# Placing a table of eight constants and padding small tables, so that every large tile of a decoder trunk starts at a multiple of 128 bytes in SBUF

## The chip, the cores and the metric

The kernel runs on one core of a Trainium2 chip. The metric is the device time of one execution in microseconds (us); the time of a kernel is the median of its runs. Five engines work side by side: TensorE (PE, whose weight loads the profile lists as PEld), VectorE (DVE), ScalarE (ACT), GpSimd (POOL) and SyncE (SP), which here only issues DMAs. SBUF is the on-chip memory; a tile takes the same byte range in each of its partitions, and all offsets below are byte offsets within a partition.

## The reference

A trunk of two layers on x of 512 tokens by 1024 features, in float32. Each layer has three post-norm steps: a SwiGLU feed-forward net (FFN), a mixer, and a second FFN.

```python
def swiglu_ffn(x, w_gu, w_down):
    a, u = jnp.split(x @ w_gu, 2, axis=-1)
    return (jax.nn.silu(a) * u) @ w_down
...
def hybrid_mixer(x, w_in, w_out, sinks, rope_cos, rope_sin, ret_cos, ret_sin):
    h = x @ w_in
    ...
    y_attn = sliding_window_sink_attention(qa, ka, va, sinks)
    ...
    y_ret = multiscale_retention(qr, kr, vr.reshape(B, S, RET_HEADS, HEAD_DIM), gr)
    return jnp.concatenate([y_attn, y_ret], axis=-1) @ w_out
...
    for l in range(DEPTH):
        x = layer_norm(DEEPNORM_ALPHA * x + 0.5 * swiglu_ffn(x, ffn1_w_gu[l], ffn1_w_down[l]),
                       ln1_g[l], ln1_b[l])
        x = layer_norm(DEEPNORM_ALPHA * x + hybrid_mixer(x, w_in[l], w_out[l], attn_sinks[l],
                                                         rope_cos, rope_sin, ret_cos, ret_sin),
                       ln2_g[l], ln2_b[l])
        x = layer_norm(DEEPNORM_ALPHA * x + 0.5 * swiglu_ffn(x, ffn2_w_gu[l], ffn2_w_down[l]),
                       ln3_g[l], ln3_b[l])
```

The hidden width of the FFN is 2816. The mixer has 8 attention heads with a window of 128 tokens and 8 retention heads, all of width 64.

## The kernel before

**Split products.** A float32 operand is split into a high part of type float32r and a low part, the rest (`split`, lines 167 to 172: ACT copies, DVE subtracts). `mm3` (lines 180 to 185) multiplies two split operands with three matmuls: high by high (L183), low by high (L184), high by low (L185), all added in one PSUM bank. In the profile's names of a matmul, `ps<-xh,uh`, the tile named first moves through the array and the second is stationary; each matmul loads its own weights.

**Tiles.** x lies transposed in `xh` and `xl` (16 KB a partition each). Weights come by DMA into two raw buffers of 8 KB and are split into units `uh` and `ul` of 4 KB, six buffers of each. `Weights` hands them out in a fixed order and loads ahead: up to six units are made before the one that PE takes. `small` holds the statistics of the norms and of attention, a few numbers a partition each.

**FFN.** For most of the 11 column blocks `glu7` forms the gate and up projections with seven products of half size instead of eight. Its moving tiles have 256 columns: slices of xh and xl in six of its 14 products, and `Th`, `Tl`, sums of slices of x, in the other eight; the units are stationary. Other blocks use `glu`, where xh moves with 256 or 512 columns. The down projection also uses seven products, in five groups of 12 matmuls each (`seventh`); there the units move with 512 columns and the hidden activations, split into xh and xl as scratch, are stationary. Between products a DMA issued on POOL (L389) adds further weights onto the tile R. A tail (`down`) takes the last two rows of blocks, with tiles `hr`, then follows `norm`.

**Mixer.** Projections as above (`proj`, `proj_tok`), then attention and retention in generators that are stepped between the matmuls of the projections, then the output projection (`half`), whose moving tiles are `b` for the first half. Transposes (L476) multiply by `ident`, which moves; so do the first matmuls of the kernel (L468, `warm`).

**Order and waits.** The order of the instructions on an engine is the program's; splits and matmuls of `mm3` are held to it. Waits between engines follow from the tiles' reads and writes. A tile of a pool waits for the last user of the buffer it takes.

**Where the tiles lie.** Pools lie one behind the other in the order in which they are opened, and each tile is rounded up to 32 bytes. `base` comes first: `ident` (512 bytes), `mhalf` (32), xh, xl, Y (16 KB each). Behind it lie the raw buffers (2 of 8 KB), the units (12 of 4 KB) and `small` (nine kinds of tile, three buffers each: 64 bytes for `st`, 32 for each other, 960 in all). Behind `small` come the pools of the stage: those of an FFN (hT, S, Th, Tl, Q, later R, hr and the tail's units), or those of the mixer, which begin with the tables: cos and sin of 2048 bytes, band 1024, causal and diag 512 each, rsc 128, `sk` and `nsk` 32 each. All other tiles have sizes that are multiples of 128 bytes.

`mhalf` holds the exponent -0.5 eight times. It is written once (L119) and read by POOL for the inverse square roots of the norms (L508) and of retention (L1086). `sk` holds the eight sinks of a layer, `nsk` their negatives; attention reads them in L989 and L991.

Of the kernel before, what the change touches and what calls it, by code (L numbers as in the profile page):

```python
# [7 lines left out]
F32 = mybir.dt.float32  # L8
# [10 lines left out]
P = 128  # L19
# [27 lines left out]
class Weights:  # L47


    def __init__(self, T, items):  # L50
        self.T, self.items = T, items
        self.emitted = self.taken = self.out = 0
        self.ready = []
        self.raws = {}
        self.last = {raw: i for i, (raw, _, _, _) in enumerate(items)}
# [44 lines left out]
class Trunk:  # L100
    def __init__(self, tc, ctx):
        self.tc, self.nc = tc, tc.nc
        self.n = 0
        self.now = 0
        self.pin = True
        self.tasks = []
        self.later = []
        self.pace = None
        self.halves = 2
        nc = self.nc  # L110
        self.base = ctx.enter_context(tc.tile_pool(name="base", bufs=1))
        self.rawp = ctx.enter_context(tc.tile_pool(name="rawp", bufs=2))
        self.unit = ctx.enter_context(tc.tile_pool(name="unit", bufs=UBUFS))
        self.small = ctx.enter_context(tc.tile_pool(name="small", bufs=3))
        self.psum = ctx.enter_context(tc.tile_pool(name="psum", bufs=8, space=PSUM))
        self.ident = self.base.tile([P, P], F32, name="ident")
        make_identity(nc, self.ident)
        self.mhalf = self.base.tile([P, 8], F32, name="mhalf")
        nc.vector.memset(self.mhalf, -0.5)  # L119
        self.xh = self.base.tile([P, KC, SEQ], F32R, name="xh")  # L120
        self.xl = self.base.tile([P, KC, SEQ], F32R, name="xl")
        self.Y = self.base.tile([P, NT, D], F32, name="Y")
# [688 lines left out]
    def mixer(self, sinks, cst, g, b):  # L811
        nc, tc, W = self.nc, self.tc, self.W
        with ExitStack() as ctx:
            cp = self.cpool = ctx.enter_context(tc.tile_pool(name=self.nm("mixc"), bufs=1))
            pool = self.mpool = ctx.enter_context(tc.tile_pool(name=self.nm("mix"), bufs=1))
            self.c = {}
            c = self.c

            def const(name, tag=None):
                ap = cst[name]  # L820
                c[name] = cp.tile(list(ap.shape), F32, tag=tag or name, name=self.nm(name))
                nc.sync.dma_start(c[name], ap)
# [2 lines left out]
            const("ropeS", "sin")  # L825
            for name in ("band", "causal", "diag", "rsc"):
                const(name)
            sk = c["sk"] = cp.tile([P, 8], F32, name=self.nm("sk"))
            nc.sync.dma_start(sk, sinks.partition_broadcast(P))
            c["nsk"] = cp.tile([P, 8], F32, name=self.nm("nsk"))  # L830
            nc.vector.tensor_scalar_mul(c["nsk"], sk, -1.0)

            self.kT = [self.tmp("qk", 6, F32R) for _ in range(2)]
# [354 lines left out]
```

## Time and profile before

| what | value |
|---|---|
| median of 3 runs | 1766.99 us |
| lowest, highest run | 1766.74, 1767.35 us |
| profiled execution, span from first to last instruction | 1765.1 us |
| mean granted TensorE clock in the span | 0.998 |
| instructions in the span | 29166 |
| HBM read, written | 212.38 MB, 2.10 MB |

The time of the profiled execution that the profile gives is its span; the runs' times also hold what lies around it. The page gives the busy time of each engine, groups of instructions by line with count, busy time and mean duration of one, and the chain of work that ended last. Durations of successive matmuls overlap on PE, so the mean duration of one is not the time that each adds. A view of all engines by stretches shows the course of the work: gate and up projections until about 220 us, down projection until about 340, mixer until about 560, then the second FFN, and the same again for the second layer.

### The profile page before, as it was taken

How to read it: one execution, taken by the hardware profiler on the slowest of the kernel's cores; microseconds unless marked ns; L12 is line 12 of the kernel's file. 1: busy time of each engine (PE TensorE's matmuls, PEld its weight loads, DVE VectorE, ACT ScalarE, POOL GpSimd, SP SyncE). 2: the span in 40 equal slices, each digit the busy share in tenths (PEclk: the TensorE clock that was granted, in tenths of full speed). 3: DMA queues.
4: the chain of work that ended last, by engine and by line, in shares of the span. 5: the costliest groups of instructions: out<-in, count | busy, mean ns of one | idle time of the engine just before them, and what ended most of it. 6: DMA issues, size and time to landing. Idle time of an engine off the chain costs nothing.

```text
span 1765.1 us, 29166 instructions
## 1 busy us (share of the span) xinstructions
PE 1752.7 (99%) x11930; PEld 1600.5 (91%) x11930; DVE 1414.9 (80%) x1975; ACT 928.1 (53%) x1456; POOL 182.9 (10%) x152
## 2 busy tenths in 40 slices
PE   9999999999999999999999999999999999999998
PEld 9999988887789999998899999889877899999886
DVE  7888888856767888878888888888567587888887
ACT  5455556378712455555535555554795234555561
POOL 0000022111111000014000000311011110000131
PEclk9999999999999999999999999999999999999999
DMA  6234389422222243369423334982233122334891
GB/s 191 97 96 133 131 202 199 131 85 88 73 79 72 74 137 102 97 208 214 140 68 99 121 96 147 211 203 91 85 95 96 48 95 97 97 96 132 211 218 48
DMA packets 163765, 216.34 MB, mean 123 GB/s; under 512 B 5168, under 2 KB 116528, under 8 KB 163632
## 3 DMA queue, kind: packets, MB, share of 16 engines
q1 hardware_dynamic: 141872, 172.55, 30.5%
q0 software_dynamic: 21760, 41.95, 13.1%
q8 instruction: 93, 1.52, 0.3%
q14 instruction: 40, 0.33, 0.1%
HBM read 212.38 MB, written 2.10 MB: 122 GB/s over the span
## 4 chain that ended last, share of the span: by engine, by line
PE 90%; issue 6%; DMA 1%; DVE 1%; POOL 1%; ACT 0%; SPq 0%; POOLq 0%; DVEq 0%
PE ps L183 29%; PE ps L185 29%; PE ps L184 29%; PE ps L476 1%; DMA raw<-in_ffn_w_gu_dram 1%; POOL sw L959 1%; PE ps L1067 1%; PE ps L1015 0%; PE ps L1029 0%; PE ps L1063 0%; PE ps L1050 0%; DMA retS<-c_retS_dram 0%; ACT sw L957 0%; DVE ul L169 0%; PE ps L1007 0%
## 5 line engine op out<-in xcount | busy, mean ns | idle before, releaser
L183 PE MATMUL ps<-xh,uh 128*128 128x256 f32 (+1 forms) x1616 | 482.2, 298 | 0.0
L185 PE MATMUL ps<-xh,ul 128*128 128x256 f32 (+1 forms) x1616 | 479.3, 297 | 1.0 <-DVE ul L169 0.9
L184 PE MATMUL ps<-xl,uh 128*128 128x256 f32 (+1 forms) x1616 | 478.5, 296 | 0.3 <-DVE xl L169 0.3
L168 ACT CAST uh<-raw 128x1024 fp32r<-128x1024 f32 (+1 forms) x274 | 237.1, 886 | 245.6 <-PE ps L184 140.1
L169 DVE TENSOR_TENSOR ul<-raw,uh 128x1024 fp32r<-128x1024 f32 (+1 forms) x274 | 273.3, 1013 | 62.2 <-ACT uh L168 61.6
L183 PE MATMUL ps<-Th,uh 128*128 128x256 f32 x1152 | 319.1, 277 | 0.0
L184 PE MATMUL ps<-Tl,uh 128*128 128x256 f32 x1152 | 318.7, 277 | 0.0
L185 PE MATMUL ps<-Th,ul 128*128 128x256 f32 x1152 | 318.3, 276 | 0.0
L185 PEld LDWEIGHTS ps<-xh,ul 128*128 128x128 f32 x1616 | 307.9, 191 | 10.1 <-DVE ul L169 1.6
L183 PEld LDWEIGHTS ps<-xh,uh 128*128 128x128 f32 x1616 | 307.9, 191 | 9.7 <-issue 1.6
L184 PEld LDWEIGHTS ps<-xl,uh 128*128 128x128 f32 x1616 | 308.0, 191 | 7.9 <-DVE xl L169 0.5
L183 PE MATMUL ps<-uh,xh 128*128 128x512 f32 x720 | 283.4, 394 | 0.5 <-ACT xh L168 0.5
L185 PE MATMUL ps<-uh,xl 128*128 128x512 f32 x720 | 280.8, 390 | 0.0
L184 PE MATMUL ps<-ul,xh 128*128 128x512 f32 x720 | 280.3, 389 | 0.0
L168 ACT CAST uh<-S 128x1024 fp32r<-128x1024 f32 x144 | 151.1, 1049 | 149.0 <-PE ps L184 145.2
L169 DVE TENSOR_TENSOR ul<-S,uh 128x1024 fp32r<-128x1024 f32 x144 | 175.9, 1222 | 60.1 <-ACT uh L168 59.5
L184 PEld LDWEIGHTS ps<-Tl,uh 128*128 128x128 f32 x1152 | 216.7, 188 | 0.0
L183 PEld LDWEIGHTS ps<-Th,uh 128*128 128x128 f32 x1152 | 216.6, 188 | 0.0
L185 PEld LDWEIGHTS ps<-Th,ul 128*128 128x128 f32 x1152 | 216.4, 188 | 0.0
L389 POOL DMA_DIRECT2D R<-in_ffn_w_down_dram x80 | 97.1, 1217 | 1020.7 <-DVE ul L169 930.0
L169 DVE TENSOR_TENSOR ul<-R,uh 128x1024 fp32r<-128x1024 f32 x120 | 145.1, 1221 | 25.8 <-ACT uh L168 25.7
L183 PEld LDWEIGHTS ps<-uh,xh 128*128 128x128 f32 x720 | 135.2, 188 | 30.1 <-issue 1.6
(143 smaller groups left out, 2362.4 us busy)
## 6 DMA issues: line engine op xcount, KB each, us to landing
raw<-in_ffn_w_gu_dram SPq DMA_DIRECT2D x86, 1024.0 KB, 5.5
R<-in_ffn_w_down_dram POOLq DMA_DIRECT2D x80, 512.0 KB, 7.6
raw<-in_w_in_dram SPq DMA_DIRECT2D x18, 1024.0 KB, 5.2
R<-in_ffn_w_down_dram SPq DMA_DIRECT2D x16, 1024.0 KB, 6.3
raw<-in_ffn_w_down_dram SPq DMA_DIRECT2D x12, 1024.0 KB, 7.2
R<-in_ffn_w_down_dram SPq DMA_DIRECT2D x8, 512.0 KB, 4.3
raw<-in_w_in_dram SPq DMA_DIRECT2D x8, 512.0 KB, 6.1
raw<-in_w_out_dram SPq DMA_DIRECT2D x8, 512.0 KB, 6.4
```

The source lines that it names most:

```text
L168: a = self.nc.scalar.copy(hi, src)
L169: b = self.low = self.nc.vector.tensor_sub(lo, src, hi.bitcast(F32))
L183: keep(mm(out, ah, bh, start=start, stop=False, **kw))
L184: keep(mm(out, ah, bl, start=False, stop=False, **kw))
L185: keep(mm(out, al, bh, start=False, stop=stop, **kw))
L389: self.nc.gpsimd.dma_start(src, rows(i, j, g * 2, 2), accum_op=ALU.add))
L476: nc.tensor.transpose(b[:, c * P : (c + 1) * P], src[:, c * P : (c + 1) * P], self.ident)
L959: nc.gpsimd.tensor_mul(sw[:, :n], sw[:, :n], S)
L1067: ins = nc.tensor.matmul(ob[:, o0 : o0 + HD], ST[h][:, n, :], vr[:, n, p * P + h * HD : p * P + (h + 1) * HD], start=n == 0, stop=n == 0 o ...
```

## The change

`mhalf` leaves the pool `base` for the pool `small`, with one buffer of its own and 16 floats (64 bytes) instead of 8. `sk` and `nsk` are taken 16 floats wide, of which the first 8 are used. Counted from the start of `ident`, xh then lies at 512 bytes instead of 544; `small` has 1024 bytes instead of 960; the mixer's tables from rsc on take 256 bytes instead of 192. Everything else is the same text.

```diff
@@ -115,7 +115,7 @@
         self.ident = self.base.tile([P, P], F32, name="ident")
         make_identity(nc, self.ident)
-        self.mhalf = self.base.tile([P, 8], F32, name="mhalf")
+        self.mhalf = self.small.tile([P, 16], F32, tag="mhalf", name="mhalf", bufs=1)
         nc.vector.memset(self.mhalf, -0.5)
         self.xh = self.base.tile([P, KC, SEQ], F32R, name="xh")
...
@@ -825,9 +825,9 @@
             for name in ("band", "causal", "diag", "rsc"):
                 const(name)
-            sk = c["sk"] = cp.tile([P, 8], F32, name=self.nm("sk"))
+            sk = c["sk"] = cp.tile([P, 16], F32, name=self.nm("sk"))[:, :8]
             nc.sync.dma_start(sk, sinks.partition_broadcast(P))
-            c["nsk"] = cp.tile([P, 8], F32, name=self.nm("nsk"))
+            c["nsk"] = cp.tile([P, 16], F32, name=self.nm("nsk"))[:, :8]
             nc.vector.tensor_scalar_mul(c["nsk"], sk, -1.0)
```

## The prediction

> **What bounds the kernel now.** I read the page's first part, then the chain that ended last, then what PE waited for.
>
> ```profile
> PE 1752.7 (99%) x11930; PEld 1600.5 (91%) x11930; DVE 1414.9 (80%) x1975; ACT 928.1 (53%) x1456; POOL 182.9 (10%) x152
> ...
> PE 90%; issue 6%; DMA 1%; DVE 1%; POOL 1%; ACT 0%; SPq 0%; POOLq 0%; DVEq 0%
> ```
>
> ```profile
> PE ps L468 <- POOL ident masks.py:199: 1.4, 1, 1.4
> PE ps L185 <- DVE ul L169: 0.9, 2, 0.7
> ```
>
> PE is busy for 1752.7 of 1765.1 us, and its longest wait is 1.4 us. Nothing starves TensorE: the time is the sum of the distances from one matmul's start to the next one's (the pitch). A change that adds and removes no instruction can move the time only by moving a pitch. Three groups make up nearly all of it; L184 and L185 have the same counts as L183, so each row stands for three.
>
> ```profile
> L183 PE MATMUL ps<-xh,uh 128*128 128x256 f32 x1408 | 398.5, 283 | 0.0
> L183 PE MATMUL ps<-Th,uh 128*128 128x256 f32 x1152 | 319.1, 277 | 0.0
> L183 PE MATMUL ps<-uh,xh 128*128 128x512 f32 x720 | 283.4, 394 | 0.5 <-ACT xh L168 0.5
> L183 PE MATMUL ps<-xh,uh 128*128 128x512 f32 x208 | 83.6, 402 | 0.0
> L183 PE MATMUL ps<-b,yah 128*128 128x512 f32 x64 | 25.3, 396 | 0.0
> L183 PE MATMUL ps<-uh,hr 128*128 128x512 f32 x64 | 25.2, 394 | 0.0
> L183 PE MATMUL ps<-uh,uh 128*128 128x512 f32 x32 | 12.5, 389 | 0.0
> ```
>
> The tile named first is the moving one, streamed through the array; the second is the stationary one. The durations (283, 277, 394 ns) overlap, so they are no pitch. The pitch is read from starts, in the timeline of PE:
>
> ```profile
> 101.80 0.28 PE L183 MATMUL ps<-xh,uh 128*128 128x256 f32 x1
> 101.92 0.28 PE L184 MATMUL ps<-xl,uh 128*128 128x256 f32 x1
> 102.04 0.28 PE L185 MATMUL ps<-xh,ul 128*128 128x256 f32 x1
> ...
> 107.28 0.28 PE L183 MATMUL ps<-Th,uh 128*128 128x256 f32 x1
> ...
> 107.62 0.28 PE L183 MATMUL ps<-Th,uh 128*128 128x256 f32 x1
> ...
> 280.67 0.39 PE L183 MATMUL ps<-uh,xh 128*128 128x512 f32 x1
> ...
> 281.35 0.39 PE L183 MATMUL ps<-uh,xh 128*128 128x512 f32 x1
> ...
> 319.22 0.39 PE L185 MATMUL ps<-uh,hr 128*128 128x512 f32 x1
> ...
> 319.90 0.39 PE L185 MATMUL ps<-uh,hr 128*128 128x512 f32 x1
> ```
>
> Two matmuls of the same 256 columns differ: 120 ns when xh or xl moves, but 0.34/3 = 113.3 ns when Th or Tl moves. With 512 columns it is 0.68/3 = 226.7 ns, from either pool. In units of 6.667 ns these are 18, 17 and 34, where 256 columns in sixteens (64 bytes each) make 16 and 512 make 32. So the array seems to take 16 columns (64 bytes a partition) per unit, and each matmul pays one or two units too many.
>
> Where the tiles lie explains surplus units. Counted from `ident`, taken as a multiple of 128 bytes, `mhalf` (32 bytes) puts xh, xl and every uh and ul of the unit pool 32 bytes past such a multiple. The small pool (960 bytes) puts the FFN pools, with Th and Tl, 96 past. The 32 bytes of `sk` and of `nsk` put the mixer's tiles back at 32. A run of 1024 bytes from offset 32 touches 9 blocks of 128 bytes, which is 18 units, as xh shows; 2048 bytes touch 17, which is 34 units, as shown too. Th at 96 pays 17 units, which are the 17 blocks of 64 bytes that it touches: the rule is not fully settled, but every pitch is what a misaligned run could cost.
>
> **The change part by part.** Nothing is issued more or less: the same memset (L119), the same two DMAs of 8 floats, the same matmuls. `mhalf` is read by 32 POOL instructions.
>
> ```profile
> L508 POOL TENSOR_TENSOR rs<-ve,mhalf 128x1 f32<-128x1 f32 x24 | 36.7, 1530 | 273.0 <-DVE ve L506 273.0
> L1086 POOL TENSOR_TENSOR gvar<-gvar,mhalf 128x8 f32<-128x8 f32 x8 | 13.1, 1642 | 74.6 <-DVE gvar L1085 74.6
> ```
>
> They read the same constants at another address; I cost that, the padding and the two wider tiles at nothing. If each were 10% longer, that would be 5 us in all, under PE's work but for the last few norms (under 1 us). Having a buffer of its own that is never taken again, `mhalf` adds no wait to any queue.
>
> What moves is the offset of xh, xl, Y, raw, uh, ul, hT, Th, Tl and all mixer tiles: all go to 0 past a multiple of 128 bytes. No large matmul of the trace has an aligned moving tile, so its pitch is bounded from rows. The surplus units gone and nothing fixed left, 256 columns take 16 x 6.667 = 106.7 ns and 512 take 213.3. The nearest rows are those whose moving tile is `ident`, the one aligned tile: transposes (L476) and plain float32 matmuls (L468), 128 columns each.
>
> ```profile
> 328.49 0.87 PE ps L476 x8
> ```
>
> ```profile
> 6.33 0.61 PE L468 MATMUL ps<-ident 128*128 128x128 f32 x4
> 6.78 0.49 PE L476 MATMUL ps<-ident,Y 128*128 128x128 f32 x3
> ```
>
> The transposes follow each other at 0.87/8 = 109 ns, the float32 matmuls at 0.45/4 = 112 ns. If they spend 16 units as well, a fixed 2.3 and 5 ns remain. The difference I put down to the weight load, 140 ns for a transpose and 188 to 192 for a matmul of either kind:
>
> ```profile
> L476 PEld LDWEIGHTS ps<-ident,Y 128*128 128x128 f32 x192 | 22.1, 142 | 2.0 <-DMA Y<-in_x_dram 0.6
> L183 PEld LDWEIGHTS ps<-Th,uh 128*128 128x128 f32 x1152 | 216.6, 188 | 0.0
> ```
>
> So for 256 columns, where every matmul loads new weights, I take the slower row, 111.7 ns. For 512 columns the load is hidden, and I take 213.3 + 2.3 = 215.6. The sum:
>
> - xh, xl moving, 256 columns: 3 x 1408 = 4224 matmuls x (120.0 - 111.7) = 35.1 us
> - Th, Tl moving: 3 x 1152 = 3456 x (113.3 - 111.7) = 5.5 us
> - 512 columns: 3 x (720 + 208 + 64 + 64 + 32) = 3264 x (226.7 - 215.6) = 36.2 us
>
> Together 76.8 us. Its bounds: 122.9 us with nothing fixed left (4224 and 3264 x 13.3, 3456 x 6.67), about 98 us if 256 columns also reach the transposes' 109; at the other end minus 23 us (below).
>
> The Trainium skill ("TensorE: Matmul & The Clock Gate", Back-to-back issue gap) gives N/2.4 + 2.5 ns for back-to-back warm matmuls, so 109 and 216 ns. The trace differs at 120, 113.3 and 226.7 ns; if alignment were the whole difference, that rule would make the saving about 96 us.
>
> **What is late next.** With PE 4% faster, its suppliers must keep up.
>
> ```profile
> 1012.00:1056.00 44.00, 44.00 (x381) 44.00 (x380) 38.74 (x60) 23.75 (x36) 0.00 (x0) 1.00 0.33 104
> ...
> 396.00:440.00 44.00, 44.00 (x254) 34.15 (x253) 27.66 (x53) 39.37 (x97) 4.03 (x4) 1.00 0.26 82
> ```
>
> A row has the stretch, its length, then PE, PEld, DVE, ACT and POOL with their counts, clock and DMA. In the gate stage DVE is the closest, 38.74 of 44 us. The 44 us shrink to about 44 x 111.7 / 116.2 = 42.3, so DVE reaches 92%: still cover. In attention ACT has 39.37 of 44, which shrink by at most 11/227, to 41.9: 94%. In the down projection it is the adding DMA:
>
> ```profile
> 266.46 1.21 POOL L389 DMA_DIRECT2D R<-in_ffn_w_down_dram  x1 [1.34 <-issue]
> 269.00 1.22 POOL L389 DMA_DIRECT2D R<-in_ffn_w_down_dram  x1 [1.33 <-DVE hT L712]
> ```
>
> They leave at 2.54 us each, while a group of 12 matmuls takes 12 x 226.7 = 2.72 us now and 2.59 then. It just fits, with 2% to spare instead of 7%. The cost of new waits lies between nothing and the whole gain of that stage, 7 products x 5 groups x 12 plus 48 in the tails, in four FFNs, 1872 matmuls x 11.1 = 20.8 us; the six unit buffers ahead of PE speak for the lower end, and I take 4 us.
>
> So 76.8 - 4 = 72.8 us. The span was 1765.1 us and the median of the runs 1766.99, 1.9 us that lie around it and stay: 1766.99 - 72.8, about 1694 us.
>
> **The rivals.**
>
> *Half the surplus stays (20%).* xh's extra unit over Th may come not from its own offset but from moving and stationary tile lying at the same offset: xh against uh 32 and 32, Th against uh 96 and 32, and all 512-column pairs alike (32 and 32, or 96 and 96). A clash would cost one unit per matmul, misalignment the other. After the change all pairs are alike, and only misalignment goes: xh 18 to 17, 512 columns 34 to 33, Th trades one for the other. That saves (4224 + 3264) x 6.67 = 50 us: 1717 us. For it: it explains 17 for Th and 34 in both pools without an exception. Against it: a clash should depend on addresses within the tiles too, and uh and ul cycle through six buffers at one pitch.
>
> *No effect (20%).* 17 units per 256 columns and 34 per 512 is one ratio, 17/16, and could be how this format streams whatever its address; xh's 18th unit would be a clash of regions that padding doesn't change. Time 1767. Against it: two equal shapes at two addresses differ by 6.7 ns. The Trainium skill ("SBUF — State Buffer", Specifications) speaks for this rival: it gives SBUF lines of 16 bytes, and offsets 32 and 96 are whole multiples of that. The pitches' common step of 6.667 ns rather goes with 64 bytes; no run here yet separates the two.
>
> *Slower (9%).* The ratio 17/16 is the format's, and the one unit between xh and Th is the clash of equal offsets, priced at 6.67 ns. Then the change only takes Th out of its lucky place: Th against uh goes from 96 and 32 to 0 and 0, its pitch from 113.3 to 120. That is 3456 x 6.67 = 23 us: 1790 us. It decides from the point where the others keep 226.7 and 120.
>
> **How the numbers follow.** The forecast has 48%, half the surplus 20%, no effect 20%, slower 9%; 3% is left for waits that eat the gain (counted as slower or same). The forecast's own range is 1669 (256 columns at 109, no waits) to 1711 (all 20.8 us lost). The range reaches from 1669 up to no effect, 1768, and leaves out the slower rival and the 1644 of no fixed part. About 0.2% (3.5 us) is what a measurement here can tell from nothing: faster 0.69, within 0.2% 0.21, slower 0.10.
>
> **What would show it.** In the timeline of PE three starts each: 512 columns at 0.65 instead of 0.68 us for three, xh and Th both near 0.335. At 0.66 and 0.34 it is the second case; xh at 0.12 and 512 at 0.68 mean no effect, and Th at 0.12 with them the slower one. PE's waits should stay under some 10 us; waits on ul or uh in the down projection would show that the DMA has become the bound. The prediction is wrong if pitches fall and the span doesn't, or if the pitches depend on what I took as fixed.

## The result, and the profile after

The changed kernel takes 1789.84 us, the median of four runs (1789.31 to 1790.23), against 1767.17 us for the kernel before in four runs. The ratio is 1.0128, with a 95% interval of 1.0114 to 1.0142: slower by 22.7 us. The profiled execution's span went from 1765.1 to 1787.7 us, by 22.6. All ratios below go by executions at a granted clock of 0.998 or 0.999; one of the four executions of split ran at 0.85, took 1915.72 us and is left out.

The page of the kernel after, busy time of the engines:

```profile
PE 1776.1 (99%) x11930; PEld 1623.9 (91%) x11930; DVE 1414.8 (79%) x1975; ACT 927.9 (52%) x1456; POOL 181.7 (10%) x152
```

The longest waits of PE in the kernel after:

```profile
PE ps L468 <- POOL ident masks.py:199: 1.4, 1, 1.4
PE ps L1029 <- DVE rr L1032: 0.9, 2, 0.4
```

The counts are those of before, DVE, ACT and POOL have the same work to do, and PE still waits for nothing. Only PE and its weight loads are busy for longer, each by some 23 us. So the matmuls themselves became slower. The groups of the kernel after, with different shapes kept apart, tell which (busy time, then mean ns of one):

```profile
L183 PE MATMUL ps<-xh,uh 128*128 128x256 f32 x1408 | 399.3, 284 | 0.0
...
L183 PE MATMUL ps<-Th,uh 128*128 128x256 f32 x1152 | 326.0, 283 | 0.0
...
L183 PE MATMUL ps<-uh,xh 128*128 128x512 f32 x720 | 283.4, 394 | 0.5 <-ACT xh L168 0.5
```

The group in which Th moves went from 319.1 to 326.0 us, 6.9 more. The group with xh (398.5 before) moved by 0.8 us, the 512-column group (283.4) not at all. Busy times of matmuls that overlap do not add up, so the shares of the 22.6 us are taken from the starts of all matmuls in both traces: those with Th or Tl moving take 21.0 us more (a mean of 120.0 ns instead of 113.9), those with 256 columns of xh or xl 1.1 us more, all others together 0.5. The mean of 113.9 before is above the 113.3 of a steady stretch because the first three pitches after each change from xh to Th were about 121, 121 and 116 ns. The starts on the timeline of PE in the kernel after show the pitch:

```profile
107.21 0.28 PE L183 MATMUL ps<-Th,uh 128*128 128x256 f32 x1
...
107.57 0.28 PE L183 MATMUL ps<-Th,uh 128*128 128x256 f32 x1
```

```profile
283.84 0.39 PE L183 MATMUL ps<-uh,xh 128*128 128x512 f32 x1
...
284.52 0.39 PE L183 MATMUL ps<-uh,xh 128*128 128x512 f32 x1
```

Three matmuls with Th or Tl moving take 0.36 us, so 120 ns each instead of 113.3. Three with 512 columns still take 0.68 us. The course of the gate stage says the same in one number. These are the rows of 88 to 220 us in the view by stretches, for PE alone, of the kernel before and of the one after: stretch, length, busy time with the count of matmuls, clock, DMA.

```profile
88.00:220.00 132.00, 132.00 (x1138) 1.00 0.37 119
```

```profile
88.00:220.00 132.00, 132.00 (x1102) 1.00 0.34 110
```

In the same 132 us, always busy and at full clock, PE starts 1102 matmuls instead of 1138: a mean pitch of 119.8 instead of 116.0 ns.

### The profile page after: what moved, and what is told of

It reads as the page before. It is cut to its first block, busy times and chain, and to the rows that moved or that the text cites. A ratio compares the mean times of both kernels' runs of the same rounds, so it can differ in the third digit from the quotient of the medians.

```text
span 1787.7 us, 29166 instructions
## 1 busy us (share of the span) xinstructions
PE 1776.1 (99%) x11930; PEld 1623.9 (91%) x11930; DVE 1414.8 (79%) x1975; ACT 927.9 (52%) x1456; POOL 181.7 (10%) x152
## 4 chain that ended last, share of the span: by engine, by line
PE 90%; issue 6%; DMA 1%; DVE 1%; POOL 1%; ACT 0%; SPq 0%; POOLq 0%; DVEq 0%
PE ps L183 29%; PE ps L185 29%; PE ps L184 29%; PE ps L476 1%; DMA raw<-in_ffn_w_gu_dram 1%; POOL sw L959 1%; PE ps L1067 1%; PE ps L1015 0%; PE ps L1029 0%; PE ps L1063 0%; PE ps L1050 0%; DMA retS<-c_retS_dram 0%; ACT sw L957 0%; DVE ul L169 0%; PE ps L1007 0%
## 5 line engine op out<-in xcount | busy, mean ns | idle before, releaser
L183 PE MATMUL ps<-Th,uh 128*128 128x256 f32 x1152 | 326.0, 283 | 0.0
L184 PE MATMUL ps<-Tl,uh 128*128 128x256 f32 x1152 | 326.0, 283 | 0.0
L185 PE MATMUL ps<-Th,ul 128*128 128x256 f32 x1152 | 326.0, 283 | 0.0
L183 PE MATMUL ps<-uh,xh 128*128 128x512 f32 x720 | 283.4, 394 | 0.5 <-ACT xh L168 0.5
L183 PEld LDWEIGHTS ps<-Th,uh 128*128 128x128 f32 x1152 | 221.2, 192 | 0.0
L184 PEld LDWEIGHTS ps<-Tl,uh 128*128 128x128 f32 x1152 | 221.2, 192 | 0.0
L185 PEld LDWEIGHTS ps<-Th,ul 128*128 128x128 f32 x1152 | 221.2, 192 | 0.0
L168 ACT CAST uh<-R 128x1024 fp32r<-128x1024 f32 x120 | 125.1, 1051 | 72.6 <-DMA R<-in_ffn_w_down_dram 34.1
```

Of the source, the lines that this page charges most:

```text
L168: a = self.nc.scalar.copy(hi, src)
L183: keep(mm(out, ah, bh, start=start, stop=False, **kw))
L184: keep(mm(out, ah, bl, start=False, stop=False, **kw))
L185: keep(mm(out, al, bh, start=False, stop=stop, **kw))
```

## The experiments

Two theories stood after the result. By the first, what counts is the **distance** of the stationary tile from the moving one: before, Th and uh lay at different offsets; after the change all pairs lie at equal offsets, and equal offsets clash. By the second, what counts is the **own offset** of the moving tile. Below, "distance" means the start of the stationary tile minus that of the moving one, modulo 256 bytes. xh against uh had distance 0 in both kernels; Th against uh had 64 before and has 0 after.

### Th pushed 64 bytes the other way (th64)

```diff
 (against the kernel after)
-        self.mhalf = self.small.tile([P, 16], F32, tag="mhalf", name="mhalf", bufs=1)
+        self.mhalf = self.small.tile([P, 32], F32, tag="mhalf", name="mhalf", bufs=1)
```

xh, uh and ul keep their places, at multiples of 128; Th and Tl lie 64 bytes further, which makes their distance minus 64.

> The table gets 32 floats (128 bytes) in the small pool, so that the FFN's own pools, Th and Tl among them, lie at 64 past a multiple of 128 bytes, while xh, xl, uh and ul stay at 0. Theory 1 (clash of equal offsets: 256 columns cost 120.0 ns where moving and stationary tile lie at the same offset within 128 bytes, 113.3 ns where they lie 64 apart): Th at 113.3 ns, xh at 120.0, 3456 x 6.67 = 23 us less than the changed kernel, about 1767 us, the same as the kernel before. Theory 2 (the moving tile's own offset counts, 96 is fast, 0 and 32 are slow): 64 is new to it; if 64 is slow, 1790 us.

It took 1783.36 us, a ratio of 1.0095 (1.0080 to 1.0110) to the kernel before. PE's timeline:

```profile
107.01 0.28 PE L183 MATMUL ps<-Th,uh 128*128 128x256 f32 x1
...
107.72 0.28 PE L183 MATMUL ps<-Th,uh 128*128 128x256 f32 x1
```

Six pitches take 0.71 us: 118 ns, neither the 113.3 of before nor the 120 of after. The first theory as it was put, 113.3 ns where the two lie 64 bytes apart, was wrong: the sign counts.

### The units pushed 64 bytes away from everything that moves (u64)

```diff
 (against the kernel after)
-        self.mhalf = self.small.tile([P, 16], F32, tag="mhalf", name="mhalf", bufs=1)
-        nc.vector.memset(self.mhalf, -0.5)
 ...
         self.Y = ...
+        self.mhalf = self.base.tile([P, 16], F32, name="mhalf")
+        nc.vector.memset(self.mhalf, -0.5)
```

The raw buffers and the units lie 64 past a multiple of 128; xh, and with it Th, lie at 0. Both now have the distance 64 that Th alone had before.

> The table of 64 bytes lies behind Y in the base pool, so that the raw buffers and the units uh and ul lie at 64, while xh, xl, Th and Tl lie at 0. Theory 1 (clash of equal offsets): both xh and Th are 64 away from the units, all 4224 + 3456 matmuls of 256 columns run at 113.3 ns instead of 120.0, 51 us less than the changed kernel, about 1739 us, ratio to the kernel before about 0.984. With 512 columns nothing changes (226.7 ns) if the weight load's clash is hidden there; if it isn't, they fall to 220 ns and another 22 us go. Theory 2 (own offset of the moving tile): xh and Th lie at 0 as in the changed kernel and stay at 120.0 ns, 1790 us.

It took 1750.99 us (1750.85 to 1757.42), a ratio of 0.9920 (0.9903 to 0.9937): faster than both kernels, though not the 1739 us that the theory gave. One of its four executions took 1757.42 us, and no trace shows why. The same stretch by count, then groups by shape:

```profile
88.00:220.00 132.00, 132.00 (x1167) 1.00 0.39 126
```

```profile
L183 PE MATMUL ps<-xh,uh 128*128 128x256 f32 x1408 | 391.3, 278 | 0.0
...
L183 PE MATMUL ps<-uh,xh 128*128 128x512 f32 x720 | 285.4, 396 | 0.5 <-ACT xh L168 0.5
...
L183 PE MATMUL ps<-xh,uh 128*128 128x512 f32 x208 | 84.5, 406 | 0.0
```

1167 matmuls in 132 us are a mean of about 113 ns, over xh and Th together. The clash that xh always had is gone there: its group fell from 398.5 to 391.3 us. But the gain is smaller than the full 6.7 ns on all 4224 matmuls (28 us), for two reasons. The groups with 512 columns became dearer (283.4 to 285.4 and 83.6 to 84.5 us, and the like on the other lines), which the theory had not foreseen; by the starts that is 7.4 us. And by the starts xh's pitch has a mean of 115.5 ns, not 113.3. In the gate stages, between stretches of Th, it is 113.3; at the start of the mixers and of three of the four FFNs it is 117.8 for stretches of tens of us, as in these rows of u64's timeline:

```profile
352.01 0.28 PE L183 MATMUL ps<-xh,uh 128*128 128x256 f32 x1
...
354.13 0.28 PE L183 MATMUL ps<-xh,uh 128*128 128x256 f32 x1
```

18 pitches take 2.12 us, 117.8 ns each. This is taken up again under micro3.

### Everything 64 bytes further, distances kept (s96)

```diff
 (against the kernel before)
-        self.mhalf = self.base.tile([P, 8], F32, name="mhalf")
+        self.mhalf = self.base.tile([P, 24], F32, name="mhalf")
```

> The kernel before with a table of 96 bytes instead of 32 in its old place: xh, xl, uh and ul lie at 96, Th and Tl at 32, every tile 64 further than before. Theory 1 (only the distance between the two tiles counts): the same as the kernel before, 1767 us, xh at 120.0 and Th at 113.3 ns. Theory 2 (own offset of the moving tile, 96 fast, 32 slow): xh at 113.3 and Th at 120.0 ns, 28 us less and 23 us more than before, 1762 us.

It took 1767.31 us, a ratio of 1.0002 (0.9993 to 1.0012), and PE's timeline shows xh at three pitches in 0.36 us, 120 ns, and Th at 12 pitches in 1.36 us, 113.3 ns, both as before:

```profile
101.06 0.28 PE L183 MATMUL ps<-xh,uh 128*128 128x256 f32 x1
...
101.42 0.28 PE L183 MATMUL ps<-xh,uh 128*128 128x256 f32 x1
...
106.56 0.28 PE L183 MATMUL ps<-Th,uh 128*128 128x256 f32 x1
...
107.92 0.28 PE L183 MATMUL ps<-Th,uh 128*128 128x256 f32 x1
```

Th lies at 32 here, where xh lay before at 120 ns, and is fast; xh lies at 96, where Th lay, and takes 120. So the own offset of the moving tile is not the cause, and the second theory falls.

### Matmuls alone, at chosen offsets (micro)

Behind the warm-up the kernel after got runs of 24 matmuls in float32r, both operands slices of xh, whose results nobody reads. The offsets below are bytes past two places that are multiples of 128 and a multiple of 256 apart. One pair of runs was in bf16, with moving and stationary slice at equal offsets too. The first run, of 72 matmuls, let the clock come up. Shortened to the float32r runs, the code is:

```python
def run(n, m, s):            # n columns; moving slice at byte m, stationary at s
    b = T.ps()
    for i in range(24):
        nc.tensor.matmul(b[:, :n], sv[:, s // 4 : s // 4 + 128], mv[:, m // 4 : m // 4 + n], start=True, stop=True)
```

> The changed kernel with some 900 matmuls put ahead of its work, whose results nobody reads: runs of 24 matmuls on two rows of xh each, with the moving slice at one offset and the stationary slice at another, a transpose between the runs. In order: 256 columns (72 times) at 0 and 0; 256 columns with the stationary at 0, 16, 32, 48, 64, 80, 96, 112 bytes; the same eight with 512 columns; for offsets 32, 64, 96 of the moving slice: 256 columns with equal offset, 256 and 512 with 64 apart; 256 columns at 0 with a stationary of 64 columns at 0 and at 64, the same with 512 columns; 256 columns with the stationary alternating between 0 and 64, then 0, 0, 64; bf16 operands with 256 and with 512 columns. Theory 1: 120.0 ns at equal offsets and 113.3 at 64 apart, whatever the moving offset; in between either, which shows how wide the clash is. If the clash is with the weight load, a stationary of half as many columns is at 113.3 or lower at both offsets. If 17/16 comes with float32r, bf16 runs at 107 to 109 and 213 to 216 ns, and 512 columns of float32r stay at 226.7 at every offset. Theory 2: 120.0 at moving offset 0 and 32, 113.3 at 96, whatever the stationary.

PE's timeline merges equal matmuls into one row: start, time from the first start to the last end, how many. One matmul of 256 columns lasts 0.28 us in float32r and 0.27 in bf16, one of 512 columns 0.39 and 0.38, so the pitch is the row's time less one matmul, divided by the count less one. These are pieces from within the runs, taken after the first few matmuls, which differ. The last column of the table is the mean of a run's last eleven pitches.

```profile
15.36 1.72 PE L1109 MATMUL ps<-xh 128*128 128x256 f32 x13
...
42.88 2.89 PE L1109 MATMUL ps<-xh 128*128 128x512 f32 x12
...
65.15 3.90 PE L1109 MATMUL ps<-xh 128*128 128x512 f32 x16
...
90.14 1.86 PE L1109 MATMUL ps<-xh 128*128 128x256 f32 x15
...
101.80 1.81 PE L1109 MATMUL ps<-xh 128*128 128x256 f32 x14
...
105.19 4.06 PE L1109 MATMUL ps<-xh 128*128 128x512 f32 x17
...
121.55 1.87 PE L1109 MATMUL ps<-xh 128*64 128x256 f32 x15
...
124.65 1.83 PE L1109 MATMUL ps<-xh 128*64 128x256 f32 x14
...
144.44 1.80 PE L1109 MATMUL ps<-bt 128*128 128x256 bf16 x15
...
147.81 3.40 PE L1109 MATMUL ps<-bt 128*128 128x512 bf16 x15
```

| row at | what runs (moving / stationary offset) | pitch by the row | by the starts, steady |
|---|---|---|---|
| 15.36 | 256 columns, 0 / 0 | 1.44 / 12 = 120 ns | 120.0 |
| 42.88 | 512 columns, 0 / 0 | 2.50 / 11 = 227 ns | 226.6 |
| 65.15 | 512 columns, 0 / 64 | 3.51 / 15 = 234 ns | 233.1 |
| 90.14 | 256 columns, 32 / 96 | 1.58 / 14 = 113 ns | 113.4 |
| 101.80 | 256 columns, 64 / 0 | 1.53 / 13 = 118 ns | 117.7 |
| 105.19 | 512 columns, 64 / 0 | 3.67 / 16 = 229 ns | 229.2 |
| 121.55 | 256 columns, 64 stationary columns, 0 / 0 | 1.59 / 14 = 114 ns | 113.3 |
| 124.65 | the same, 0 / 64 | 1.55 / 13 = 119 ns | 119.1 |
| 144.44 | bf16, 256 columns, 0 / 0 | 1.53 / 14 = 109 ns | 109.2 |
| 147.81 | bf16, 512 columns, 0 / 0 | 3.02 / 14 = 216 ns | 215.8 |

Outside the kernel the clash is the same. Equal offsets give 120.0 ns at 0, 32, 64 and 96; the stationary slice 64 ahead of the moving one gives 113.3, and 64 behind 117.7. For 512 columns it is the other way round: equal offsets are best. And at aligned, equal offsets float32r takes 226.6 ns where bf16, at equal offsets too, takes 215.8. **That 5% remains where alignment and distance are the same: it goes with the operands' type.** For bf16 the Trainium skill ("TensorE: Matmul & The Clock Gate", Back-to-back issue gap) gives N/2.4 + 2.5 ns, as the gap of an isolated matmul on a warm clock, so 109.2 and 215.8: the trace agrees to the decimal. The prediction had held the same rule against float32r, whose steady pitch no run here brings below 113.3 and 226.6.

Two forecasts for these runs failed: 113.3 ns at any 64 bytes apart, where the pairs with the stationary slice 64 behind take 117.7, and 226.7 ns for 512 columns at every offset, where only equal offsets have it. With the stationary slice at the other multiples of 16 up to 112, 256 columns take 117.9 to 120.0 ns and 512 take 231.8 to 234.5. Stationary slices that alternate between 0 and 64 give 118.3, and 0, 0, 64 in turn 117.7.

With half as many stationary columns the same moving stream meets a shorter weight load (135 ns in the profile instead of 192), and the places change: 0 / 0 gets the 113.3 and 0 / 64 the 119.1. The forecast for a clash with the weight load, 113.3 or less at both offsets, failed at 0 / 64. That the pitch changes at all with the length of the load speaks for the weight load as the other party of the clash; whether by what it reads or by when it reads, these runs don't tell.

### Aligned or not, clash or not (mis0, al64)

The change moved two things, alignment and distance. These two fill in the missing cells. mis0 leaves xh and the units at 32, as before, and lengthens the small pool by an unused tile of 64 bytes, which brings Th to 32 too (its lines count one more):

```diff
 (mis0, against the kernel before)
         self.Y = ...
+        self.small.tile([P, 16], F32, tag="pad", name="pad", bufs=1)
```

> The kernel before with 64 unused bytes in the small pool: xh, xl, uh and ul stay 32 past a multiple of 128 bytes, and Th and Tl come to 32 as well, so nothing large is aligned and the distance from Th to the units is 0. Theory 1 (the distance from the moving to the stationary tile sets the pitch of 256 columns: 0 gives 120.0 ns, +64 gives 113.3, -64 gives 117.7): Th at 120.0 ns, 3456 x 6.67 = 23 us more than before, 1790 us. Rival (alignment itself is slow): the same as before, 1767 us.

al64 aligns xh and the units to 128 as the change does, but leaves the small pool at 960 bytes:

```diff
 (al64, against the kernel after)
+        self.mhalf = self.base.tile([P, 32], F32, name="mhalf")
+        nc.vector.memset(self.mhalf, -0.5)
         self.ident = self.base.tile([P, P], F32, name="ident")
 ...
-        self.mhalf = self.small.tile([P, 16], F32, tag="mhalf", name="mhalf", bufs=1)
-        nc.vector.memset(self.mhalf, -0.5)
```

> The changed kernel with the table, 128 bytes now, ahead of ident: xh, xl, uh and ul stay at multiples of 128 bytes (of 256 for the units), and the FFN's pools with Th and Tl come 64 bytes lower against them, so that a Th slice's stationary tile lies +64 from it. In the run before this one the pools lay 64 higher, at -64. Theory 1 with its sign: Th at 113.3 ns, 23 us less than the changed kernel, 1767 us, the same as the kernel before. If only the amount counts and not the sign: 117.7 ns as in that run, 1783 us. Rival (alignment itself is slow): near 1790 us.

The timeline of PE in mis0, then in al64:

```profile
106.52 0.28 PE L184 MATMUL ps<-Th,uh 128*128 128x256 f32 x1
...
107.96 0.28 PE L184 MATMUL ps<-Th,uh 128*128 128x256 f32 x1
```

```profile
106.57 0.28 PE L183 MATMUL ps<-Th,uh 128*128 128x256 f32 x1
...
107.25 0.28 PE L183 MATMUL ps<-Th,uh 128*128 128x256 f32 x1
...
107.94 0.28 PE L183 MATMUL ps<-xh,uh 128*128 128x256 f32 x1
...
108.30 0.28 PE L183 MATMUL ps<-xh,uh 128*128 128x256 f32 x1
```

In mis0 Th takes 1.44/12 = 120 ns. In al64 it takes 0.68/6 = 113.3, while xh, aligned as well, stays at 0.36/3 = 120.

| | Th at distance 64 | Th at distance 0 |
|---|---|---|
| xh and units 32 past a multiple of 128 | before: 1767 us | mis0: 1789.98 us, ratio 1.0132 (1.0117 to 1.0148) |
| xh and units at a multiple of 128 | al64: 1766.10 us, ratio 0.9996 (0.9987 to 1.0006) | after: 1789.84 us, ratio 1.0128 (1.0114 to 1.0142) |

Along a row the time changes by 23 to 24 us, along a column by nothing that can be told. By the starts Th and Tl take 21.0 us more than before in mis0, as in the changed kernel, and 0.0 more in al64. So being at a multiple of 128 instead of 32 past one costs nothing and brings nothing here; the distance of Th from the units makes the result.

### Two views of x (split)

u64 lost time on 512 columns, which want distance 0, and gained on 256, which want 64. In split both halves of x lie in one tile with two views 64 bytes apart: the first one moves in the 256-column products, the second serves as stationary operand of the down and output projections.

```diff
 (against the kernel before; mhalf moves ahead of ident)
-        self.xh = self.base.tile([P, KC, SEQ], F32R, name="xh")
-        self.xl = self.base.tile([P, KC, SEQ], F32R, name="xl")
+        E = KC * SEQ
+        xx = self.base.tile([P, 2 * E + 16], F32R, name="xx")
+        self.xh, self.xl, self.zh, self.zl = (xx[:, o : o + E].rearrange("p (k t) -> p k t", k=KC)
+                                              for o in (0, E, 16, E + 16))
 ...
-                hh, hl = (v[:, k : k + f, h * 256 : (h + 1) * 256] for v in (self.xh, self.xl))
+                hh, hl = (v[:, k : k + f, h * 256 : (h + 1) * 256] for v in (self.zh, self.zl))
 ...
-                self.to_xT(gates[t], t, 0)
+                self.to_xT(gates[t], t, 0, (self.zh, self.zl))
 ...
-                yh, yl = (self.xh, self.xl) if part else self.ya
+                yh, yl = (self.zh, self.zl) if part else self.ya
```

The last 64 bytes of a row of the second view lie over the first 16 tokens of the next row of x, so those values of x are changed and the result is not that of the reference; the instructions and their shapes are the same.

> xh and xl in one tile with two views: the one that x is kept in, and a second one 64 bytes further, which holds the down projection's and the output projection's stationary operands. Units lie +64 from the first view and 0 from the second, Th and Tl are as the first view. Theory 1: the 7680 matmuls with 256 columns at 113.3 ns, and those with 512 columns whose units move (2160 of 3264) back at 226.7, where the run with the units 64 further had 226 to 232. That run was at 1751 us; its 512-column starts summed to 7.4 us more than before, of which some 5 us should come back: 1746 us. If the second view makes new waits: 1751 us or more.

The ratio is 0.9905 (0.9887 to 0.9923); the three executions took 1747.37 (the profiled one), 1748.37 and 1753.87 us, where 1746 was forecast. Its groups by shape, with both halves of x now named xx and line numbers two higher:

```profile
L185 PE MATMUL ps<-xx,uh 128*128 128x256 f32 x1408 | 390.8, 278 | 0.1
...
L185 PE MATMUL ps<-uh,xx 128*128 128x512 f32 x720 | 283.9, 394 | 0.5 <-ACT xx L170 0.5
...
L185 PE MATMUL ps<-xx,uh 128*128 128x512 f32 x208 | 84.5, 406 | 0.0
```

The down projection is back at 283.9 us from u64's 285.4 (by the starts, its three lines take 3.0 us less than in u64), and the gate products keep their gain; the 208 in which x moves with 512 columns still lie at distance 64 and stay at 84.5. So the rule, 64 for 256 columns and 0 for 512, works in the kernel too. Against u64 it is worth some 3 us, with intervals that overlap. A version in which the rows of x have room for both views was not tried.

### More offsets (micro2, micro3)

The same isolated runs with more offsets: micro2 mostly with the moving slice at 0 and the stationary one at up to 320 bytes, micro3 a grid of eight moving by eight stationary offsets, 32 bytes apart, then the pairs at distance 64 a second time in falling order.

> As the first run of matmuls by themselves, other offsets. In order: 256 columns at 0 and 0 (72 times); moving at 0, stationary at 0, 32, 64, ... 288; then moving and stationary at 64 and 128, 96 and 160, 96 and 32, 192 and 0, 128 and 192, 0 and 576, 128 and 128; then 512 columns, moving at 0, stationary at 0, 64, 128, 192, 256, 320; then 256 columns, stationary at 0, 64, 128, 192 again. Theory 1, distance modulo 256: 113.3 ns at +64 whatever the moving offset (64 and 128, 96 and 160, 128 and 192, 192 and 0, 0 and 576), 117.7 at 96 and 32 and at stationary 192, 120.0 at 256, 118.1 at 288, 128 is open. Rival 1 (the moving slice must lie in the lower 64 bytes): 117.7 at 64 and 128, 96 and 160. Rival 2 (what ran before decides which of two pitches is kept): the last four differ from the same offsets at the start.

> The changed kernel with 1,960 matmuls of 256 columns ahead of its work, whose results nobody reads, in runs of 24 (the first of 72) with a transpose between: a grid of the moving slice at 0, 32, ... 224 bytes by the stationary slice at 0, 32, ... 224, the stationary fastest; then the pairs 256 and 64, 256 and 320, 352 and 160, 448 and 0, 448 and 512, 224 and 288, 192 and 256; then +64 (modulo 256) for the moving slice at 224 down to 0. Theory 1 as first put (only the distance modulo 256 counts) is out for moving offsets of 96 and more, where +64 gave 117.8 ns. Theory 1b (the pair of places modulo 256 counts): 120.0 on the whole diagonal, 113.3 at +64 for 0, 32 and 64, 117.8 at +64 for 96, 128 and 192, the same on the way back down, and 256 and 64 as 0 and 64. Rival (what ran before decides): the way down differs from the grid. Which other cells are fast is open.

In micro2 three pairs at distance 64 (96 / 160, 128 / 192 and 192 / 0) took 117.8 ns and three others 113.3 or 113.4, so the first theory, by which the distance alone sets the pitch, does not hold in full. All the float32r runs of 256 columns in micro3's grid, by distance (mean of the last eleven pitches):

| distance, bytes | pitch in the eight cells, ns |
|---|---|
| 0 | 120.0 in all |
| 32 | 118.3 to 118.7 |
| 64 | 113.3 or 113.4 in five, 117.7 to 117.8 in three |
| 96 | 117.3 to 120.0 |
| 128 | 118.5 to 120.1 |
| 160 | 119.5 to 120.4 |
| 192 (minus 64) | 117.7 to 117.8 |
| 224 | 116.5 to 117.9 |

In micro2 the pattern repeats after 256 bytes: 256 columns take 120.0 ns at 0 and at 256; 512 columns take 226.7 and 226.6 at distances 0 and 256, 228.9 at 192, and 233.0 to 233.5 at 64, 128 and 320. At 256 columns, distance 64 has not one pitch but two. These rows of micro3's timeline are the pair 0 / 64 in the grid and, later in the same execution, once more:

```profile
25.21 1.86 PE L1109 MATMUL ps<-xh 128*128 128x256 f32 x15
```

```profile
248.25 1.93 PE L1109 MATMUL ps<-xh 128*128 128x256 f32 x15
```

The same addresses and the same instructions give 1.58/14 = 113 ns the first time and 1.65/14 = 118 the second. Four of the eight pairs changed sides between the two passes, and each run keeps its pitch to its end once it is steady. This also ends the theory that the pair of places modulo 256 decides. So at distance 64 two steady courses exist, and not the addresses alone pick one; something that went before is the likeliest, but it was not isolated. Where Th lay at distance 64 it kept the fast course in all kernels here; xh in u64 and split shows both, which is where their mean of about 115 ns comes from. What picks the course was not settled.

## Why the prediction was wrong

**What bounds the kernel** was read rightly: PE is always busy, waits for nothing, and the time moved with the pitch, nearly all of it (21.0 of 22.6 us) with that of one group.

**The step that failed** is "each matmul pays one or two units too many", with the alignment as its reason: "every pitch is what a misaligned run could cost". The pitches of 17 and 34 units are what float32r takes at the best offsets tried, aligned or not; only xh's 18th unit is a surplus, and it comes from equal offsets of moving and stationary tile. micro showed the first (226.6 ns at 0 / 0, against 215.8 in bf16), the four cells with mis0 and al64 the second. The prediction had noted that Th at 96 did not fit its block rule and went on.

**The terms of the sum.** 35.1 us for xh and xl: nothing came, since xh and uh stayed at equal offsets, 120 ns. 5.5 us for Th and Tl: a loss of 21.0 instead, from 113.3 to 120 in steady stretches. 36.2 us for 512 columns: nothing, 226.7 stays. The bounds for an aligned matmul came from rows of another kind, transposes and plain float32 matmuls of 128 columns; float32r with 256 columns did not follow them. The 4 us for new waits had nothing to meet, since PE became slower.

**The edits at nothing.** POOL's work went from 182.9 to 181.7 us with `mhalf` elsewhere, and PE's waits stayed at 1.4 us and less: right. **What is late next** was never put to the test by the change, since PE became slower. In u64, with PE 16 us faster in the span, PE's waits still add up to no more than 1.4 us for any releaser; but its down projection had become slower, so the adding DMA was not pressed there either.

**The rivals.** "Slower" had the mechanism: the ratio 17/16 as the format's, the clash at equal offsets, Th taken "out of its lucky place", 23 us and 1790 us, against 22.7 and 1789.84 measured. That the total fits so closely is in part luck: its one term was 21.0 us, and 1.6 us came from groups that it did not count. It got 9%, and the range ended at 1768 and left it out. Its clash had been doubted because it "should depend on addresses within the tiles too, and uh and ul cycle through six buffers at one pitch". But these steps are 4096 bytes between units, 512 between stationary slices and 1024 between moving ones, all multiples of 256, so the cycling changes no distance modulo 256. The steps could be had from the layout; that the pattern repeats every 256 bytes was shown by micro2 only. "Half the surplus stays" shared the clash but took one unit of misalignment as given, for which nothing is found. "No effect" was right on 17/16 and on xh under this change, and missed Th; its clash "that padding doesn't change" did change with u64's padding. The Trainium skill's line of 16 bytes ("SBUF — State Buffer", Specifications), named beside that rival, fits in that going from 32 past a multiple of 128 to 0 changed nothing; no run here has an offset off a multiple of 16.

**What would show it** was rightly set: "Th at 0.12 with them the slower one", and that is what the timeline shows.

## What to carry to other kernels

Where TensorE is the bound and two equal shapes have two pitches, look at the distance between moving and stationary operand before the alignment of either: here 64 bytes of padding in the right place are worth 0.8%, and in the wrong place cost 1.3%. For float32r with 256 moving and 128 stationary columns, the stationary tile 64 bytes ahead of the moving one (modulo 256) has the lowest pitch measured, in its fast course, and equal offsets are nearly the worst; with 512 columns equal offsets are best. Two dozen isolated matmuls for each offset, put ahead of the kernel, measure it in one run; the first ten or so are not steady yet.

## What the runs showed of the hardware that was not expected

- The pitch of float32r matmuls with 256 columns depends on the distance between moving and stationary operand: 120.0 ns at distance 0, 113.3 or 117.8 at 64, 117.8 at minus 64, and with 64 stationary columns 113.3 at 0 and 119.1 at 64. The Trainium skill ("SBUF — State Buffer", Who interferes with whom) gives PE two independent read ports, one for the moving operand and one for the weight load, and says that PE never waits on anyone; a pitch that depends on the distance of the two operands does not look like independent reads. Which part of the path the two share was not shown.
- float32r takes 226.6 ns for 512 columns at the best offsets tried where bf16 takes 215.8 at equal ones. Whether that is the format or its twice as many bytes a column, no run here separates.
- At distance 64 two steady courses exist, 113.3 and 117.8 ns, for the same instructions at the same addresses.
